# Three halves of an adaLN conditioning, from TensorE's products to GpSimd's multiplies and adds

## The chip, the cores and the metric

The kernel is one program on one NeuronCore of a Trainium2 chip. The metric is the time of one execution on the device in microseconds (us), the median of several runs. Besides, one execution was recorded by the hardware profiler, which gives each engine's instructions with their start and duration. The engines are TensorE (PE), VectorE (DVE), ScalarE (ACT), GpSimd (POOL) and SyncE (SP), which only starts DMA transfers here. Each has a queue of its own that it works off in order; an instruction that has to wait for another engine or a transfer holds up all that stands behind it in its queue.

## The reference

A decoder trunk with two layers, 256 tokens, 1024 features, one sequence, float32. Each layer has a mixer (layer 0: two kinds of softmax attention, groups A and B, of eight heads each) and a gated FFN, both between norms. What the layers add is set by a conditioning vector c: for each layer one product of 1024 x 6144 gives six vectors of 1024.

```python
cond = jax.nn.silu(c)                                     # 1 x 1024
for layer in range(DEPTH):
    mod = cond @ ada_w[layer] + ada_b[layer]              # 1 x 6144
    shift_m, scale_m, gate_m, shift_f, scale_f, gate_f = [m[:, None, :] for m in jnp.split(mod, 6, axis=-1)]
    h = rmsnorm(x, mix_pre_g[layer]) * (1.0 + scale_m) + shift_m
    y = even_mixer(h, ...) if layer % 2 == 0 else odd_mixer(h, ...)
    x = x + gate_m * rmsnorm(y, mix_post_g[layer])
    h = rmsnorm(x, ffn_pre_g[layer]) * (1.0 + scale_f) + shift_f
    y = conv_ffn(h, ffn_w_up[layer], ffn_conv_w[layer], ffn_conv_b[layer], ffn_w_down[layer])
    x = x + gate_f * rmsnorm(y, ffn_post_g[layer])
```

The 24 MB of `ada_w` of a layer are read once, for a product with a single row.

## The kernel before

The weights of the conditioning are worked off in halves of 512 columns. A half is named by its first column: 2048 and 2560 are gate_m, 3072 and 3584 shift_f, 4096 and 4608 scale_f, 5120 and 5632 gate_f. One half is four transfers of 128x2x512 (512 KB each, `ada_load`, L143, tiles aw_2048_0 to aw_2048_3), so eight row tiles of 128x512. The tiles go through a pool `aw` of four buffers: a load waits until the reader of the tile four before has finished. Only 5632 has buffers elsewhere (tag `qkv`).

There are two ways to work off a half. By products (p, `ada_main`, L151): eight matmuls, each with a padded conditioning column cpad (128x32) as weights, four row groups of TensorE side by side; each takes two passes, so that the profile counts 16; ScalarE then copies the rows out (L158, or L270 for a gate). On VectorE (v, `ada_sum`, L195 and L197): the first row tile times its 128 values of the conditioning, then seven times multiply and add in one operation, into acc, which keeps a sum for each partition. Either way, a shift or scale is turned by four transposes on TensorE (L167) so that a feature has a partition of its own, reduced over the rest by VectorE (L168) and gets its bias (L171) and gain (L174): `ada_keep`, which writes mod. A gate is needed on all partitions: one matmul with a matrix of ones (L272) sums it and spreads it, and VectorE multiplies the gain on (L274).

Which half is worked off how and behind which point of the program stands in the table ADA_AT; `more_ada(point)` is called behind each pair of heads and each projection. Halves of kind v are put on a list, and `step_aside` issues a few of their steps at a time between VectorE's other work. The gate of the FFN, 5120 and 5632, is not in the table: its products fill TensorE's waits at the boundary between mixer and FFN (`gate_halves`, L276).

The boundary (`boundary`, L375 to L464) takes the mixer's result y0m, two tiles of 128 tokens by two halves of features. For the first token tile: squares on ScalarE (L331), root on GpSimd (L335, L336: rpm); VectorE multiplies with the gate (ygm, L388), adds it to the trunk (xr, L392); squares and root again (rnm); xnm (L406); TensorE turns it (xTm, L414); ScalarE and VectorE apply scale and shift (hsm, L422 and L424), and the result is split into two parts hh (L427) and hl (L431). The same for the second token tile, interleaved. The first product of the FFN is u (L473), with weights rawu that are split by ScalarE and VectorE (L311, L312) into wu.

The order of the instructions on each engine is set when the program is built, by a scheduler that plays the program through with estimated times and takes what is ready first. Inside the boundary the order of VectorE, ScalarE, GpSimd and TensorE is as the lines are written, yet steps of the conditioning may be scheduled between them. SP's order is as written for the first part of the program, and set by the scheduler from the attention on.

## Time and profile before

| | |
|---|---|
| median of 3 runs | 692.56 us |
| fastest, slowest run | 691.07, 694.53 us |
| span of the profiled execution | 690.2 us |
| busy, TensorE / VectorE | 672.1 us / 525.3 us |
| busy, ScalarE / GpSimd | 369.8 us / 32.7 us |

The span runs from the first to the last instruction of the profiled execution. The profile gives no other time of that execution than its span. Layer 0's attention lies between about 60 and 161 us, the boundary in front of the FFN between 161 and 176 us, and the FFN of layer 0 from there on. The granted clock of TensorE is 1.00 in all the stretches shown below, the higher of its two levels.

### The profile page before, as it was taken

Reading aid. Unit: us, or ns where it says so; the run is one execution under the profiler, and the core shown is the slowest. Engines: PE = TensorE matmul, PEld = TensorE weight load, DVE = VectorE, ACT = ScalarE, POOL = GpSimd, SP = SyncE. Lnnn points to the kernel's source line nnn. Section 1 sums busy time; section 2 is a strip of 40 time slices with the busy share of each in tenths; the row PEclk is TensorE's granted clock in tenths of the full one; section 3 lists DMA queues with packets and bytes.
Section 4 is the critical chain, followed back from the end, with each engine's and each line's share of the span. In section 5 each row is a group of like instructions: output and inputs, shape, how many; then the busy total and the mean of one; then the engine's idle time right before and its main releaser. Section 6 shows DMA issues by size and latency. Waiting matters only on the chain.

```text
span 690.2 us, 11782 instructions
## 1 busy us (share of the span) xinstructions
PE 672.1 (97%) x4547; PEld 573.6 (83%) x4547; DVE 525.3 (76%) x1008; ACT 369.8 (54%) x645; POOL 32.7 (5%) x95
## 2 busy tenths in 40 slices
PE   8899999999999999999999999999999999999996
PEld 6667986476899999999986998767599999999994
DVE  1553577688899999999978787774788777777775
ACT  3433464835565555555655645864565555555552
POOL 2000000001000000000001002410200000000000
PEclk9999999999999999999999999999999999999998
DMA  7999986996858878888875867622266555555511
GB/s 256 352 368 360 221 307 240 326 348 223 294 194 290 277 257 297 264 258 277 285 270 184 290 225 266 210 82 88 75 190 237 185 183 183 183 184 188 191 49 62
DMA packets 100819, 159.12 MB, mean 231 GB/s; under 512 B 4087, under 2 KB 62611, under 8 KB 100763
## 3 DMA queue, kind: packets, MB, share of 16 engines
q1 hardware_dynamic: 100739, 158.35, 69.2%
q8 instruction: 36, 0.59, 0.3%
q14 instruction: 20, 0.16, 0.1%
q10 hardware_dynamic: 24, 0.02, 0.0%
HBM read 156.52 MB, written 1.84 MB: 229 GB/s over the span
## 4 chain that ended last, share of the span: by engine, by line
PE 88%; DVE 5%; ACT 2%; DMA 1%; issue 1%; POOL 1%; SPq 1%; DVEq 0%; POOLq 0%; ACTq 0%
PE u L473 36%; PE y1f L688 9%; PE y0f L688 9%; PE psb L473 3%; PE psd L473 3%; PE y1m L688 2%; PE y0m L688 2%; PE psa_q L809 2%; PE psa_k L809 2%; PE ada_first L151 2%; PE ada L151 1%; DMA aw_first<-in_ada_w 1%; PE sab L600 1%; PE sab L592 1%; PE sab L572 1%
## 5 line engine op out<-in xcount | busy, mean ns | idle before, releaser
L737 ACT ACTIVATE cv<-u,cvT 128x256 f32<-128x256 f32 x88 | 49.1, 560 | 65.3 <-PE u L473 61.4
L473 PE MATMUL u<-hh,wu_0h 128*128 128x256 f32 x352 | 69.8, 280 | 1.2 <-DVE hh L427 1.2
L473 PE MATMUL u<-hh,wu_1h 128*128 128x256 f32 x352 | 70.0, 280 | 0.0
L473 PE MATMUL u<-hh,wu_1l 128*128 128x256 f32 x352 | 69.9, 279 | 0.0
L473 PE MATMUL u<-hh,wu_0l 128*128 128x256 f32 x352 | 69.5, 279 | 0.0
L311 ACT CAST wu_1h<-rawu 128x1024 fp32r<-128x1024 f32 x44 | 46.2, 1051 | 31.1 <-PE y1f L688 17.6
L738 DVE SCALAR_TENSOR_TENSOR cv<-u,cvT,cv 128x255 f32<-128x255 f32 x88 | 42.0, 478 | 27.1 <-ACT cv L737 27.0
L473 PEld LDWEIGHTS u<-hh,wu_0h 128*128 128x128 f32 x352 | 54.8, 188 | 4.2 <-PE ada L272 1.4
L195 DVE SCALAR_TENSOR_TENSOR acc<-aw,cpad,acc 128x512 f32<-128x512 f32 x77 | 57.6, 749 | 0.4
L312 DVE TENSOR_TENSOR wu_0l<-rawu,wu_0h 128x1024 fp32r<-128x1024 f32 x44 | 53.5, 1221 | 5.3 <-ACT wu_0h L311 5.3
L311 ACT CAST wu_0h<-rawu 128x1024 fp32r<-128x1024 f32 x44 | 46.0, 1046 | 19.0 <-PE u L473 18.9
L312 DVE TENSOR_TENSOR wu_1l<-rawu,wu_1h 128x1024 fp32r<-128x1024 f32 x44 | 53.6, 1217 | 3.0 <-ACT wu_1h L311 2.9
L473 PEld LDWEIGHTS u<-hh,wu_1h 128*128 128x128 f32 x352 | 53.7, 188 | 0.0
L473 PEld LDWEIGHTS u<-hh,wu_1l 128*128 128x128 f32 x352 | 53.7, 188 | 0.0
L473 PEld LDWEIGHTS u<-hh,wu_0l 128*128 128x128 f32 x352 | 53.5, 188 | 0.0
L473 PE MATMUL u<-hl,wu_1h 128*128 128x256 f32 x352 | 48.2, 279 | 0.0
L473 PE MATMUL u<-hl,wu_0h 128*128 128x256 f32 x352 | 48.2, 279 | 0.0
L311 ACT CAST wd_0h<-rawd 128x1024 fp32r<-128x1024 f32 x26 | 27.3, 1049 | 35.2 <-PE u L473 31.7
L473 PEld LDWEIGHTS u<-hl,wu_1h 128*128 128x128 f32 x352 | 44.2, 188 | 0.0
L473 PEld LDWEIGHTS u<-hl,wu_0h 128*128 128x128 f32 x352 | 44.2, 188 | 0.0
L740 DVE SCALAR_TENSOR_TENSOR cv<-u,cvT,cv 128x254 f32<-128x254 f32 x88 | 41.7, 477 | 1.4
L312 DVE TENSOR_TENSOR wd_0l<-rawd,wd_0h 128x1024 fp32r<-128x1024 f32 x26 | 31.7, 1221 | 13.4 <-ACT wd_0h L311 13.2
(556 smaller groups left out, 1566.0 us busy)
## 6 DMA issues: line engine op xcount, KB each, us to landing
rawu<-in_ffn_w_up SPq DMA_DIRECT2D x44, 1024.0 KB, 5.2
aw<-in_ada_w SPq DMA_DIRECT2D x80, 512.0 KB, 6.7
rawd<-in_ffn_w_down SPq DMA_DIRECT2D x22, 1024.0 KB, 5.1
aw_first<-in_ada_w SPq DMA_DIRECT2D x32, 256.0 KB, 5.1
rawaqk<-in_ab_w_in SPq DMA_DIRECT2D x8, 512.0 KB, 6.7
rawb<-in_ab_w_in SPq DMA_DIRECT2D x4, 1024.0 KB, 8.7
rawd<-in_cd_w_in SPq DMA_DIRECT2D x4, 1024.0 KB, 5.8
rawc<-in_cd_w_in SPq DMA_DIRECT2D x4, 544.0 KB
```

The source lines that it names most:

```text
L151: last_main[:] = [nc.tensor.matmul(ps[32 * j:32 * j + 32, 0:cols], cpad[:, k, :], ws[k // 2][:, k % 2, 0:cols], start=(k < 4), stop=(k >= ...
L195: nc.vector.scalar_tensor_tensor(acc, w, c_k, acc, op0=ALU.mult, op1=ALU.add)
L311: nc.scalar.copy(hi, src)
L312: low = nc.vector.tensor_tensor(lo, src, hi.bitcast(F32), op=ALU.subtract)
L473: nc.tensor.matmul(dst(f), w[:, k, f * P:(f + 1) * P], h[:, 4 * u + k, :], start=(u == 0 and first(f) and f not in seen), stop=(u == 1 and ...
L572: nc.tensor.matmul(ps[:, P:3 * P], q[:, P:S], k, start=True, stop=True)
L592: nc.tensor.transpose(self.ps[j][:, b * P:(b + 1) * P], lt[:, b * P:(b + 1) * P], ident)
L688: last_down[:] = [nc.tensor.matmul(ys[t][:, h, :], g[p // 2][:, t * P:(t + 1) * P], wu[p % 2][:, h * 512:(h + 1) * 512], start=start and p ...
L737: nc.scalar.activation(tt[:, s, :], u_ps, AF.Identity, bias=cvT[:, bcol:bcol + 1], scale=col(2))
L738: nc.vector.scalar_tensor_tensor(tt[:, s, 1:S], u_ps[:, 0:S - 1], col(1), tt[:, s, 1:S], op0=ALU.mult, op1=ALU.add)
L740: nc.vector.scalar_tensor_tensor(tt[:, s, 2:S], u_ps[:, 0:S - 2], col(0), tt[:, s, 2:S], op0=ALU.mult, op1=ALU.add)
L809: nc.tensor.matmul((pq, pk)[f // 4][:, f % 4 // 2, f % 2 * S:(f % 2 + 1) * S], w[:, f * P:(f + 1) * P], h[:, kk, :], start=(kk == 0 and f ...
```

## The change

The kind p of the table is replaced by a kind g: the eight row tiles are summed on GpSimd. GpSimd multiplies the first row tile by its conditioning column into acc; each further row tile is multiplied in place, in its aw buffer, and then added to acc: eight multiplies and seven adds of 128x512 for each half. The halves are 2048, 2560 (gate) and 3072 (shift) of layer 0. What follows is what kind v had already: the transposes and the reduction over 128 partitions, or the product with ones. The steps are issued at once, not between VectorE's work. `ada_part` and `ada_cols` go; comments go too, and with them line numbers move by up to 14.

```diff
 ADA_AT = {
-    "a0": [("p", 0, 2, 0)],
+    "a0": [("g", 0, 2, 0)],
     "a1": [("v", 0, 4, 0)],
-    "a3": [("p", 0, 2, 1), ("p", 0, 3, 0)],
+    "a3": [("g", 0, 2, 1), ("g", 0, 3, 0)],
     "bv": [("v", 0, 4, 1)],
     "b3": [("v", 0, 3, 1)],
...
-    def ada_part(layer, c0, ws):
-        ps = bank(f"ada_{layer}_{c0}", "a")
-        ada_main(ps, ws)
-        part = small(f"part_{layer}_{c0}", tag="part")
-        nc.scalar.copy(part, ps)
-        return ps, part
...
-    def ada_sum(acc, ws):
+    def ada_sum(acc, ws, engine):
         for k in range(KT):
             yield
             w, c_k = ws[k // 2][:, k % 2, :], cpad[:, k, 0:1]
-            if k:
-                nc.vector.scalar_tensor_tensor(acc, w, c_k, acc, op0=ALU.mult, op1=ALU.add)
+            if not k:
+                engine.tensor_scalar_mul(acc, w, c_k)
+            elif engine is nc.vector:
+                engine.scalar_tensor_tensor(acc, w, c_k, acc, op0=ALU.mult, op1=ALU.add)
             else:
-                nc.vector.tensor_scalar_mul(acc, w, c_k)
+                engine.tensor_scalar_mul(w, w, c_k)
+                engine.tensor_tensor(acc, acc, w, op=ALU.add)
...
-        yield from ada_sum(acc, ws)
+        yield from ada_sum(acc, ws, engine)
...
-    def ada_cols(layer, which, h, gain=None):
-        columns_for(layer, which)
-        c0 = which * D + h * 512
-        ps, part = ada_part(layer, c0, ada_load(layer, c0))
-        ada_keep(layer, which, 4 * h, ps, part, range(4), gain)
...
-        if on_vector:
+        if engine:
             brow = small(f"brow_{layer}_{c0}", (1, 512), tag="t")
             nc.scalar.dma_start(brow, ada_b[layer:layer + 1, c0:c0 + 512])
-            yield from ada_sum(part, ws)
+            yield from ada_sum(part, ws, engine)
...
         for kind, layer, which, h in ADA_AT.get(point, ()):
+            engine = nc.vector if kind == "v" else nc.gpsimd
             if which == 2:
-                gate = ada_gate(layer, which, h, mix_post_g, on_vector=kind == "v")
-                if kind == "v":
-                    aside.append(gate)
-                else:
-                    list(gate)
-                continue
-            args = (layer, which, h, {1: MIX_G, 4: FFN_G}.get(which))
+                steps = ada_gate(layer, which, h, mix_post_g, engine=engine)
+            else:
+                steps = ada_vector(layer, which, h, {1: MIX_G, 4: FFN_G}.get(which), engine)
             if kind == "v":
-                aside.append(ada_vector(*args))
+                aside.append(steps)
             else:
-                ada_cols(*args)
+                list(steps)
```

The scheduler then orders the engines anew. On SP, the loads of the conditioning in front of the boundary stood like this before (each row is a line, the tile written, its source and, in brackets, the queues and engines whose signals it waits for; DMAHW is an earlier transfer):

```order
L304 DMA rawu_0_1_1797<-in_ffn_w_up 128x8x256 [waits DMAHW1_49,DVE_49]
L143 DMA aw_4608_0_1284<-in_ada_w 128x2x512 [waits DMAHW3_49,DMAHW2_49,PE_49]
L143 DMA aw_4608_1_1286<-in_ada_w 128x2x512 [waits DMAHW4_49,PE_49]
L143 DMA aw_4608_2_1288<-in_ada_w 128x2x512 [waits DMAHW5_49,PE_49]
L143 DMA aw_4608_3_1290<-in_ada_w 128x2x512 [waits DMAHW6_49,PE_49]
L304 DMA rawu_1_0_1937<-in_ffn_w_up 128x8x256 [waits DMAHW7_49,DVE_49]
L143 DMA aw_3584_0_1616<-in_ada_w 128x2x512 [waits DMAHW3_49,DMAHW0_49,DVE_49]
L143 DMA aw_3584_1_1618<-in_ada_w 128x2x512 [waits DMAHW4_49,DMAHW1_49,DVE_49]
L143 DMA aw_3584_2_1620<-in_ada_w 128x2x512 [waits DMAHW5_49,DMAHW2_49,DVE_49]
```

and stand like this in the changed program:

```order
L290 DMA rawu_1_0_1959<-in_ffn_w_up 128x8x256 [waits DMAHW7_49,DVE_49]
L143 DMA aw_3072_1_952<-in_ada_w 128x2x512 [waits DMAHW0_49,Pool_49]
L143 DMA aw_3072_2_954<-in_ada_w 128x2x512 [waits DMAHW1_49,Pool_49]
L143 DMA aw_3072_3_956<-in_ada_w 128x2x512 [waits DMAHW2_49,Pool_49]
L143 DMA aw_5632_0_1675<-in_ada_w 128x2x512 [waits DMAHW3_49,PE_49]
L143 DMA aw_5632_1_1677<-in_ada_w 128x2x512 [waits DMAHW4_49]
L143 DMA aw_5632_2_1679<-in_ada_w 128x2x512 [waits DMAHW5_49,DVE_49]
L143 DMA aw_4608_0_1306<-in_ada_w 128x2x512 [waits DMAHW6_49,Pool_49]
L143 DMA aw_4608_1_1308<-in_ada_w 128x2x512 [waits DMAHW6_49,DMAHW0_49,DVE_49]
L143 DMA aw_5632_3_1681<-in_ada_w 128x2x512 [waits DMAHW1_49,PE_49]
L290 DMA rawu_1_1_1961<-in_ffn_w_up 128x8x256 [waits DMAHW2_49,DVE_49]
L143 DMA aw_4608_2_1310<-in_ada_w 128x2x512 [waits DMAHW3_49,Pool_49]
```

All of 4608 stood in front of 3584, waiting for TensorE; now the tiles of 3072 stand in front, waiting for GpSimd (Pool), 4608_0 waits for GpSimd and 4608_1 for VectorE. Further behind, the loads of 3584 and 5120 now wait for VectorE's sums, and the last of these is the last tile of 5120:

```order
L143 DMA aw_3584_0_1638<-in_ada_w 128x2x512 [waits DMAHW5_49,DMAHW0_49,DVE_49]
L143 DMA aw_3584_1_1640<-in_ada_w 128x2x512 [waits Pool_49]
L143 DMA aw_3584_2_1642<-in_ada_w 128x2x512 [waits DMAHW7_49,DMAHW3_49,DVE_49]
L143 DMA aw_3584_3_1644<-in_ada_w 128x2x512 [waits DMAHW4_49,DVE_49]
L143 DMA aw_5120_0_1662<-in_ada_w 128x2x512 [waits DMAHW5_49,DMAHW1_49,DVE_49]
L143 DMA aw_5120_1_1664<-in_ada_w 128x2x512 [waits DMAHW6_49,DMAHW2_49,DVE_49]
L143 DMA aw_5120_2_1666<-in_ada_w 128x2x512 [waits DMAHW7_49,DVE_49]
L143 DMA aw_5120_3_1668<-in_ada_w 128x2x512 [waits DMAHW0_49,DVE_49]
```

In before these too waited for VectorE (the first piece shows it for 3584), yet for sums that it made ahead of the boundary, and 5632 stood among them.

On VectorE, the beginning of the boundary before, from the last two sums of 3584 to the second pair of xr:

```order
L195 SCALAR_TENSOR_TENSOR acc_3584_1624<-aw_3584_3_1622,cpad,acc_3584_1624 128x512
L388 TENSOR_TENSOR ygm_0_0_1668<-y0m_0_1473,gate_2_764 128x512
L388 TENSOR_TENSOR ygm_0_1_1669<-y0m_1_1474,gate_2_764 128x512
L392 SCALAR_TENSOR_TENSOR xr<-ygm_0_0_1668,rpm_0_1678,xr 128x512
L392 SCALAR_TENSOR_TENSOR xr<-ygm_0_1_1669,rpm_0_1678,xr 128x512
L406 TENSOR_SCALAR xnm_0_0_1692<-xr,rnm_0_1689 128x512
L406 TENSOR_SCALAR xnm_0_1_1694<-xr,rnm_0_1689 128x512
L388 TENSOR_TENSOR ygm_1_0_1670<-y0m_0_1475,gate_2_764 128x512
L168 TENSOR_REDUCE mod_3_933<-ada_3584_1633 128x4
L388 TENSOR_TENSOR ygm_1_1_1671<-y0m_1_1476,gate_2_764 128x512
L171 TENSOR_TENSOR mod_3_933<-mod_3_933,vT 128x4
L392 SCALAR_TENSOR_TENSOR xr<-ygm_1_0_1670,rpm_1_1700,xr 128x512
```

and in the changed program, from ygm on, and then, eight rows further, up to the norm of the second token tile:

```order
L374 TENSOR_TENSOR ygm_0_0_1690<-y0m_0_1495,gate_2_764 128x512
L374 TENSOR_TENSOR ygm_0_1_1691<-y0m_1_1496,gate_2_764 128x512
L190 SCALAR_TENSOR_TENSOR acc_4608_1314<-aw_4608_2_1310,cpad,acc_4608_1314 128x512
L378 SCALAR_TENSOR_TENSOR xr<-ygm_0_0_1690,rpm_0_1700,xr 128x512
L378 SCALAR_TENSOR_TENSOR xr<-ygm_0_1_1691,rpm_0_1700,xr 128x512
L190 SCALAR_TENSOR_TENSOR acc_4608_1314<-aw_4608_2_1310,cpad,acc_4608_1314 128x512
L190 SCALAR_TENSOR_TENSOR acc_4608_1314<-aw_4608_3_1312,cpad,acc_4608_1314 128x512 x2
L392 TENSOR_SCALAR xnm_0_0_1714<-xr,rnm_0_1711 128x512
L392 TENSOR_SCALAR xnm_0_1_1716<-xr,rnm_0_1711 128x512
L161 TENSOR_REDUCE mod_3_949<-ada_3072_974 128x4
L188 TENSOR_SCALAR acc_3584_1646<-aw_3584_0_1638,cpad 128x512
```

```order
L190 SCALAR_TENSOR_TENSOR acc_3584_1646<-aw_3584_1_1640,cpad,acc_3584_1646 128x512
L164 TENSOR_TENSOR mod_4_829<-mod_4_829,vT 128x4
L190 SCALAR_TENSOR_TENSOR acc_3584_1646<-aw_3584_1_1640,cpad,acc_3584_1646 128x512
L167 SCALAR_TENSOR_TENSOR mod_4_829<-mod_4_829,vT 128x4
L190 SCALAR_TENSOR_TENSOR acc_3584_1646<-aw_3584_2_1642,cpad,acc_3584_1646 128x512 x2
L190 SCALAR_TENSOR_TENSOR acc_3584_1646<-aw_3584_3_1644,cpad,acc_3584_1646 128x512 x2
L161 TENSOR_REDUCE mod_3_949<-ada_3584_1655 128x4
L164 TENSOR_TENSOR mod_3_949<-mod_3_949,vT 128x4
L410 TENSOR_SCALAR hsm_0_1_1760<-xTm_0_1_1730,mod_4_829,mod_3_949 128x128 x2
L413 CAST hh<-hsm_0_0_1757 128x4x128
L392 TENSOR_SCALAR xnm_1_0_1777<-xr,rnm_1_1767 128x512
L392 TENSOR_SCALAR xnm_1_1_1779<-xr,rnm_1_1767 128x512
```

Behind ygm_0 now stand the last four sums of 4608 and all of 3584, and with them the reductions and adds that make mod_3 and mod_4; xnm_1_0, which stood behind hsm_0 and the first cast before, stands behind all of these.

On TensorE, the transposes of xnm_1_0 (xTm_1) stand behind the products of 5120 and 5632 in both programs. Before:

```order
L414 MATMUL xTm_0_0_1707<-ident,xnm_0_1_1694 128x128 x2
L414 MATMUL xTm_0_1_1708<-ident,xnm_0_1_1694 128x128 x2
L151 MATMUL ada_5120_1652<-aw_5120_0_1640,cpad 32x512 x2
L151 MATMUL ada_5120_1652<-aw_5120_1_1642,cpad 32x512 x2
L151 MATMUL ada_5120_1652<-aw_5120_2_1644,cpad 32x512 x2
L151 MATMUL ada_5120_1652<-aw_5120_3_1646,cpad 32x512 x2
L151 MATMUL ada_5632_1663<-aw_5632_0_1653,cpad 32x512 x2
L151 MATMUL ada_5632_1663<-aw_5632_1_1655,cpad 32x512 x2
L151 MATMUL ada_5632_1663<-aw_5632_2_1657,cpad 32x512 x2
L151 MATMUL ada_5632_1663<-aw_5632_3_1659,cpad 32x512 x2
L272 MATMUL ada_5120_1652<-part_5120_1650,ones 128x512
L414 MATMUL xTm_1_0_1709<-ident,xnm_1_0_1755 128x128 x2
```

and in the changed program:

```order
L160 MATMUL ada_4608_1341<-ident,acc_4608_1314 128x128 x4
L160 MATMUL ada_3584_1655<-ident,acc_3584_1646 128x128 x4
L151 MATMUL ada_5120_1674<-aw_5120_0_1662,cpad 32x512 x2
L151 MATMUL ada_5120_1674<-aw_5120_1_1664,cpad 32x512 x2
L151 MATMUL ada_5120_1674<-aw_5120_2_1666,cpad 32x512 x2
L151 MATMUL ada_5120_1674<-aw_5120_3_1668,cpad 32x512 x2
L151 MATMUL ada_5632_1685<-aw_5632_0_1675,cpad 32x512 x2
L151 MATMUL ada_5632_1685<-aw_5632_1_1677,cpad 32x512 x2
L151 MATMUL ada_5632_1685<-aw_5632_2_1679,cpad 32x512 x2
L151 MATMUL ada_5632_1685<-aw_5632_3_1681,cpad 32x512 x2
L261 MATMUL ada_5120_1674<-part_5120_1672,ones 128x512
L400 MATMUL xTm_1_0_1731<-ident,xnm_1_0_1777 128x128 x2
```

The transposes of 4608 and 3584 have come in between those of xnm_0 and the products of 5120.

## Rows read from the trace of the kernel before

**Rows 1.** The page: engine, busy us, share of the span, instructions.
```profile
PE 672.1 (97%) x4547; PEld 573.6 (83%) x4547; DVE 525.3 (76%) x1008; ACT 369.8 (54%) x645; POOL 32.7 (5%) x95
```

**Rows 2.** The page: busy tenths of GpSimd in 40 slices of 17.3 us.
```profile
POOL 2000000001000000000001002410200000000000
```

**Rows 3.** Chain of waits, 60 to 182 us: start, us, what.
```profile
92.84 1.85 PE ada L151 x16
...
120.53 1.85 PE ada L151 x16
...
130.40 1.84 PE ada L151 x12
...
132.72 0.98 PE ada L151 x4
...
172.59 0.75 POOL rnm L336
```

**Rows 4.** TensorE's timeline at the boundary: start, busy us, what, idle before.
```profile
169.36 3.64 PE L151 MATMUL ada<-aw,cpad 128*32 128x512 f32 x32 [0.43 <-DVE mod L168]
172.93 1.12 PE L272 MATMUL ada<-part,ones 128*128 128x512 f32 x2
173.90 1.09 PE L414 MATMUL xTm<-ident,xnm 128*128 128x128 f32 x8
...
176.40 0.50 PE L473 MATMUL u<-hh,wu_0h 128*128 128x256 f32 x2 [0.55 <-DVE hh L427]
```

**Rows 5.** Stretches: span; busy us (count) of PE, PEld, DVE, ACT, POOL; clock; DMA share; GB/s.
```profile
200.00:365.00 165.00, 163.27 (x1150) 151.94 (x1148) 152.96 (x264) 89.15 (x128) 1.72 (x4) 1.00 0.82 269
```

**Rows 6.** GpSimd's groups: count, busy us, mean ns, idle before.
```profile
L961 POOL TENSOR_TENSOR qt<-rpq 128x64 f32<-128x64 f32 x4 | 1.3, 320 | 1.8 <-DVE rpq L958 1.8
...
L962 POOL TENSOR_TENSOR kr<-rpk 128x16 f32<-128x16 f32 x2 | 0.4, 218 | 0.0
L883 POOL TENSOR_SCALAR_AFFINE_SELECT causal<-causal 128x256 f32<-128x256 f32 x1 | 0.4, 399 | 0.0
...
masks.py:199 POOL TENSOR_SCALAR_AFFINE_SELECT ident<-ident 128x128 f32<-128x128 f32 x1 | 0.3, 293 | 0.0
```

**Rows 7.** Line 195: count, ns min/median/max, first and last start.
```profile
L195 DVE SCALAR_TENSOR_TENSOR acc<-aw,cpad,acc x77: 727/744/889, 98.7 to 432.7; 128x512 f32<-128x512 f32 x77
```

**Rows 8.** Line 335, the same columns.
```profile
L335 POOL TENSOR_SCALAR rpf<-sspf x4: 299/300/752, 360.6 to 684.8; 128x1 f32<-128x1 f32 x4
```

**Rows 9.** SP's timeline, 125 to 165 us.
```profile
131.42 2.69 SPq L143 DMA_DIRECT2D aw<-in_ada_w  x4
...
158.07 3.92 SPq L143 DMA_DIRECT2D aw<-in_ada_w  x2
```

**Rows 10.** Tile aw, 45 to 182 us: ns min/median/max; transfers.
```profile
L195 DVE SCALAR_TENSOR_TENSOR acc<-aw,cpad,acc x21: 727/743/752, 98.7 to 160.9; 128x512 f32<-128x512 f32 x21
L197 DVE TENSOR_SCALAR acc<-aw,cpad x3: 481/482/486, 97.8 to 149.1; 128x512 f32<-128x512 f32 x3
...
DMA to landing us min/median/max: 4.1/7.0/8.6
```

**Rows 11.** VectorE's timeline at the boundary.
```profile
162.24 1.38 DVE L388 TENSOR_TENSOR ygm<-y0m,gate 128x512 f32<-128x512 f32 x2 [0.65 <-ACT junkpm L331]
163.97 1.41 DVE L392 SCALAR_TENSOR_TENSOR xr<-ygm,rpm,xr 128x512 f32<-128x512 f32 x2 [0.35 <-POOL rpm L336]
167.22 0.89 DVE L406 TENSOR_SCALAR xnm<-xr,rnm 128x512 f32<-128x512 f32 x2 [1.83 <-POOL rnm L336]
...
168.62 0.68 DVE L168 TENSOR_REDUCE mod<-ada 128x4 f32<-128x512 f32 x1
...
169.82 0.15 DVE L171 TENSOR_TENSOR mod<-mod,vT 128x4 f32<-128x4 f32 x1
...
173.36 0.88 DVE L406 TENSOR_SCALAR xnm<-xr,rnm 128x512 f32<-128x512 f32 x2 [0.45 <-POOL rnm L336]
```

More of the change, by code (lines that the diff above doesn't have):

```diff
@@ L152, in ada_main, with ada_keep @@
                                              start=(k < 4), stop=(k >= 4), tile_position=(0, 32 * j))]
-    def ada_part(layer, c0, ws):
-        ps = bank(f"ada_{layer}_{c0}", "a")
-        ada_main(ps, ws)
-        part = small(f"part_{layer}_{c0}", tag="part")
-        nc.scalar.copy(part, ps)
-        return ps, part
-    def ada_keep(layer, which, k0, ps, part, blocks, gain, per=4):
+    def ada_keep(layer, which, k0, ps, part, blocks, gain, per):
         n = len(blocks)
@@ L193, in ada_sum, with ada_vector @@
             w, c_k = ws[k // 2][:, k % 2, :], cpad[:, k, 0:1]
-            if k:
-                nc.vector.scalar_tensor_tensor(acc, w, c_k, acc, op0=ALU.mult, op1=ALU.add)
-            else:
-                nc.vector.tensor_scalar_mul(acc, w, c_k)
-    def ada_vector(layer, which, h, gain):
+            if not k:
+                engine.tensor_scalar_mul(acc, w, c_k)
+            elif engine is nc.vector:
+                engine.scalar_tensor_tensor(acc, w, c_k, acc, op0=ALU.mult, op1=ALU.add)
+            else:
+                engine.tensor_scalar_mul(w, w, c_k)
+                engine.tensor_tensor(acc, acc, w, op=ALU.add)
+    def ada_vector(layer, which, h, gain, engine):
         columns_for(layer, which)
@@ L243, in ada_first_load, with ada_gate @@
         return w
-    def ada_gate(layer, which, h, post_g, tag="aw", on="a", on_vector=False):
+    def ada_gate(layer, which, h, post_g, tag="aw", on="a", engine=None):
         c0 = which * D + h * 512
```

## The prediction

> **What bounds the kernel now.** I read the busy shares first. TensorE is busy 672.1 of 690.2 us, VectorE 525.3, GpSimd 32.7 [rows 1], and GpSimd's slices are empty from the second to the ninth, 17 to 155 us [rows 2]. Then the chain of waits, from 60 to 182 us, where the change lies. It runs on TensorE almost without a break up to 161.5 us, and the four pieces of it that carry the products of the three halves are to be seen there by their line: 1.85, 1.85, 1.84 and 0.98 us [rows 3]. So they are on the path, and a product taken away lets everything behind it move up. From 162 to 176 us the chain changes hands: ScalarE's squares, VectorE's norm and modulation, GpSimd's root [rows 3], until u, the FFN's first product, starts at 176.40 [rows 4]. That start is the figure to follow: from 200 to 365 us TensorE is busy 163.27 of 165.00 us [rows 5], and the order of the instructions there is the same in both kernels, so that a start that comes late by some microseconds has at most 1.7 us in which to be made good. The change is decided by when u starts.
>
> **What is removed.** 48 products of 128x512, 1.85 + 1.85 + 1.84 + 0.98 = 6.52 us, all on the chain [rows 3], and three copies on ScalarE, which is no part of the chain there. The product with ones of each gate, and the four transposes of the shift, stay. If nothing else moved, the time would be 692.6 - 6.5 = 686.0.
>
> **What is added on GpSimd.** 24 multiplies and 21 adds of 128x512. No row of before has either at that size. Nearest rows [rows 6]: an add-like operation of two inputs takes 0.320 us at 64 columns and 0.218 at 16, an operation of one input 0.293 at 128 and 0.399 at 256. From below: each no dearer than the largest seen, 24 x 0.40 + 21 x 0.32 = 16 us. From above: in proportion to the columns, 24 x 1.17 + 21 x 2.56 = 82 us. I take the slopes between the rows, 2.1 and 0.83 ns a column, as both rows of a pair are of one kind: an add 1.27, a multiply 0.61, 14.6 + 26.7 = 41 us in all, nearly 14 us for a half. GpSimd has from about 58 to 150 us for it and nothing else to do [rows 2], so 41 us hide beside TensorE and 82 would not.
>
> A rule speaks against this cover. In the rows, a GpSimd operation of 0.300 us takes 0.752 in the longest of its four executions, and the longest of VectorE's 77 sums 0.889 against 0.744 [rows 7, 8]: something is shared. The Trainium skill, SBUF — State Buffer, section "Who interferes with whom", says that VectorE and GpSimd share one pair of ports, held by one of them for the whole instruction. By it the 45 operations would wait behind VectorE's two-input ones, up to 0.74 us each, 33 us more; that is the case of the late GpSimd below.
>
> **What moves: the loads.** All weights of the conditioning go through four buffers (aw). TensorE empties a buffer at once; GpSimd holds each for three or four operations. The scheduler has answered this by its order. On SP, the loads of 4608 stood ahead of everything of 3584; now three tiles of 3072 wait for GpSimd in front, and 4608_0 behind the last add of 2560; the loads of 3584 and 5120 now wait for VectorE's sums of 4608 and of 3584, tile by tile. In before 4608 was issued from 131.42 on, and the last tile of 5120 in the pair that ends at 161.99 [rows 9]. By my prices GpSimd is through with 2560 at about 139 (its last multiplies wait for a tile) and with 3072 at about 149, so 4608_0 lands about 144, 4608_2 about 154.
>
> **What moves: VectorE.** In before all sums stand ahead of ygm, the first step of the boundary. Now four of 4608 and all eight of 3584 stand behind it. Sums last 0.743, the first of a half 0.482 [rows 10]: 11 x 0.743 + 0.482 = 8.66 us. In before ygm starts at 162.24 and the shift (mod) is done at 169.97, 7.73 later [rows 11]. In the new order there come into that stretch: 8.66 of sums; two more reductions, 2 x 0.68 = 1.36; their adds, 2 x 0.15 = 0.3; the second pair of xr, 1.41, and two of hsm, about 0.7, which stood behind it; and the way over TensorE's transposes, 0.6. Out of it goes the wait for rnm, 1.83, as there is work in it now; 0.35 stays [rows 11]. So the shift is done at 7.73 + 8.66 + 1.36 + 0.3 + 1.41 + 0.7 + 0.6 - 1.83 = 18.9 us after ygm, and the last sum at 17.5. xnm of the second token tile, which started 173.36 - 162.24 = 11.1 after ygm, starts at 18.9 + 0.7 + 0.4 = 20.0: 9 us more.
>
> **What moves: TensorE's wait.** In front of the transposes of that tile (xTm at 173.90, 11.66 after ygm) stand the products of the gates 5120 and 5632, 3.64 us for both, and one with ones, 0.56 [rows 4]. In before they hide under VectorE's work. Now the last tile of 5120 is issued only when the last sum of 3584 has freed its buffer, 17.5 after ygm; a tile lands 4.1 us after its issue at the least, 7.0 in the median [rows 10]; then a quarter of 5120's products, all of 5632's and the ones: 0.46 + 1.82 + 0.56 = 2.8. Transposes at 17.5 + 4.1 + 2.8 = 24.4, or 27.3 by the median: 12.7 to 15.6 us later against ygm than before. I take 13, near the lower, as SP has nothing else to send by then. Queued behind these products on TensorE are the transposes and all of the FFN, so the whole wait counts.
>
> **The sum.** ygm comes earlier by the removed 6.5 less what TensorE loses in waits for GpSimd's sums and late loads; I give that 1 us, so -5.5 (the ends are -6.5, nothing lost, and -3). The boundary grows by 13 (9 if 5120 is not late, 15.6 by the median). -5.5 + 13 = +7.5. The profiled execution has a span of 690.2 us, 2.4 under the median of the runs; no other time of it is given. 690.2 + 7.5 = 697.7 span, so 700.1 as a median: I say 700. Its own range, from -6.5 + 12 to -4.5 + 15.6, is 698 to 704.
>
> **Rivals.**
> GpSimd is late (chance 0.14). If its operations wait for VectorE as in the rows of 0.752 and 0.889, the half 3072 ends at about 160 instead of 149, as 15 operations after the last load of it cost 0.7 more each. The load of 4608_2 waits for it; VectorE needs it 1.4 us after ygm, at about 158, and would stand there until 166. Some 6 us of this is not covered: 692.6 + 7.5 + 6 = 706. For it: the two outliers [rows 7, 8]. Against it: they are the longest of 81, and GpSimd hardly ran beside VectorE in before, so the rows say little either way.
> A wash (chance 0.19). The tiles of 5120 land in time, so VectorE's 9 us alone lengthen the boundary, against -6: +3, 695.5. For it: nothing but these tiles is then on SP, and three of four are asked for earlier. Against it: even the shortest landing is 4.1 us.
> Faster (chance 0.12). VectorE absorbs its sums at the boundary. The point is between ygm and xnm: if the sums run at the start-to-start pace of a pair, 1.41 - 0.74 = 0.67, and fill the waits of 1.83, 0.35 and 0.45 [rows 10, 11], they add 11 x 0.67 + 0.4 - 2.6 = 5.2, and the reductions fall into waits for TensorE. The products give 6.5, the FFN's 1.7 us of waits come back [rows 5], and so do TensorE's 0.43 and 0.55 in front of it [rows 4]: 692.6 + 5.2 - 6.5 - 1.7 - 1.0 = 688.6. It decides for this when the boundary grows by less than 3 us, which needs the last tile of 5120 on its way within 8 us of ygm. Against it: the tile's buffer is freed by the last sum.
> That the change does nothing, because the products were hidden: against it stands that all four pieces are on the chain; its time would lie in the wash.
>
> **How the numbers follow.** Forecast 0.55, late GpSimd 0.14, wash 0.19, faster 0.12. The time is the forecast's, 700. What can be told from no change is 0.5%, 3.5 us: under 689.1 is faster, over 696.0 slower. Slower: forecast and late GpSimd, 0.69. The same: the wash, and some of the faster case that ends above 689.1, 0.21. Faster: 0.10. A range of 8 in 10 takes the wash and the forecast whole, the faster case in part and the late GpSimd up to 707: 690.5 to 707.
>
> **What would show it.** In the profile of the changed kernel: GpSimd busy about 41 us more, in two stretches before 150; no product of 2048, 2560 and 3072 on the chain; y0m and ygm 5 to 6 us earlier; between ygm and xnm on VectorE twelve sums, and the shift about 19 us after ygm; TensorE waiting first for VectorE's last sum and then some 4 us for aw before the last products of 5120; u at 183 to 184 and the FFN behind it as long as before. I am wrong if u starts before 180, if the sums of GpSimd take more than 60 us, or if the stretch from u to the end changes by more than 2 us.

## The result, and the profile after

The changed kernel takes 709.63 us (708.03 to 710.51, four runs) beside 691.82 us of the kernel before (four runs too) on the same chip: ratio 1.0242, interval 1.0211 to 1.0272. That is 17.8 us slower. I had forecast 700, in 690.5 to 707: a loss of 7.5 us.

The page of the changed kernel, with the rows that answer to [rows 1, 2], and TensorE's granted clock in the same 40 slices:

```profile
PE 672.9 (95%) x4499; PEld 575.4 (81%) x4499; DVE 538.6 (76%) x1010; ACT 368.3 (52%) x642; POOL 109.9 (16%) x140
...
POOL 2007729782000000000002000530100000000000
PEclk9999999798699999999999999999999999999999
```

GpSimd has 77.2 us more, in slices 4 to 10, and TensorE 0.8 us more [rows 1] in spite of the missing products: its granted clock falls in slices 8, 10 and 11, and a piece of a product that took 0.592 us in before takes 1.06 at the lower level (the median of the 32 pieces of 5120 and 5632). The chain of waits from the end of the attention to u (start, us, what):

```profile
143.72 1.01 DVE ltab L575
...
145.10 5.72 DMA aw<-in_ada_w
...
150.85 0.48 DVE acc L188
...
157.85 0.05 SPq L290
...
157.99 9.10 DMA aw<-in_ada_w
...
167.85 0.76 DVE xr L378
...
183.05 1.10 PE ada L160 x4
...
195.31 4.70 PE u L459 x38
```

In before the attention's end was TensorE's work, up to the last products of y0m:

```profile
158.04 3.46 PE y0m L688 x14
```

Now two transfers of aw stand in the chain, of 5.72 and 9.10 us, and TensorE comes into it again only at 183. u starts at 195.31 instead of 176.40 [rows 4], 18.9 us later, and the span is 18.6 us longer (708.8 instead of 690.2): what is lost is lost before u, and behind it only 0.3 us is given back. VectorE at the boundary, the columns as in [rows 11]:

```profile
155.19 2.31 DVE L298 TENSOR_TENSOR wo0c_1l<-rawo0c,wo0c_1h 128x1024 fp32r<-128x1024 f32 x1
...
161.78 1.37 DVE L374 TENSOR_TENSOR ygm<-y0m,gate 128x512 f32<-128x512 f32 x2
167.18 0.75 DVE L190 SCALAR_TENSOR_TENSOR acc<-aw,cpad,acc 128x512 f32<-128x512 f32 x1 [4.02 <-DMA aw<-in_ada_w]
167.85 1.41 DVE L378 SCALAR_TENSOR_TENSOR xr<-ygm,rpm,xr 128x512 f32<-128x512 f32 x2
169.17 2.32 DVE L190 SCALAR_TENSOR_TENSOR acc<-aw,cpad,acc 128x512 f32<-128x512 f32 x3
...
179.79 3.12 DVE L190 SCALAR_TENSOR_TENSOR acc<-aw,cpad,acc 128x512 f32<-128x512 f32 x4
```

ygm starts at 161.78, 0.46 us earlier than before. Right behind it the fifth sum of 4608 stands still for 4.02 us until its tile, 4608_2, has landed, and xr, whose operands were ready (GpSimd had written rpm by 163.49), waits behind it. The last sum ends at 179.79 + 3.12 = 182.91. TensorE behind it, answering to [rows 4]:

```profile
183.05 1.09 PE L160 MATMUL ada<-ident,acc 128*128 128x128 f32 x4 [7.75 <-DVE acc L190]
184.92 7.10 PE L151 MATMUL ada<-aw,cpad 128*32 128x512 f32 x32 [0.78 <-DVE mod L161]
...
192.92 1.04 PE L400 MATMUL xTm<-ident,xnm 128*128 128x128 f32 x8
...
195.31 0.50 PE L459 MATMUL u<-hh,wu_0h 128*128 128x256 f32 x2 [0.49 <-DVE hh L413]
```

The 32 pieces of the products of 5120 and 5632 take 7.10 us instead of 3.64; their weight loads (PEld) show that the last tile of 5120 came at 187.79, 4.9 us after the last sum:

```profile
186.48 0.34 PEld L151 LDWEIGHTS ada<-aw,cpad 128*32 128x32 f32 x4 [1.36 <-DMA aw<-in_ada_w]
187.79 0.19 PEld L151 LDWEIGHTS ada<-aw,cpad 128*32 128x32 f32 x6 [0.97 <-DMA aw<-in_ada_w]
```

By stretches (columns as in [rows 5]):

```profile
120.00:140.00 20.00, 15.48 (x60) 8.54 (x58) 16.02 (x57) 11.93 (x41) 15.70 (x11) 0.74 0.63 203
176.00:183.00 7.00, 0.00 (x0) 0.00 (x0) 6.80 (x13) 0.01 (x1) 0.00 (x0) 0.50 0.50 149
186.00:190.00 4.00, 4.00 (x19) 1.24 (x18) 1.92 (x5) 1.43 (x5) 0.84 (x2) 0.50 0.85 274
200.00:365.00 165.00, 165.00 (x1212) 156.25 (x1211) 155.43 (x262) 90.84 (x123) 0.00 (x0) 1.00 0.81 271
```

From 120 to 140 us, in the attention, TensorE is busy 15.48 of 20 us at a granted clock of 0.74; from 176 to 183 it does nothing, and the products from 186 to 190 run at 0.50, the lower of its two levels (1.2 GHz). The FFN is as forecast, without gaps. GpSimd's new work, shortest, median and longest in ns:

```profile
L192 POOL TENSOR_SCALAR aw<-aw,cpad x21: 1557/1577/2690, 59.1 to 146.7; 128x512 f32<-128x512 f32 x21
```
```profile
L193 POOL TENSOR_TENSOR part<-part,aw x14: 1260/1303/2327, 68.0 to 139.0; 128x512 f32<-128x512 f32 x14
L193 POOL TENSOR_TENSOR acc<-acc,aw x7: 1262/1292/2152, 125.3 to 154.3; 128x512 f32<-128x512 f32 x7
```

An add takes 1.26 to 1.30 us, as I had it (1.27); a multiply takes 1.56 at its shortest, where I had 0.61.

### The profile page after: what moved, and what is told of

The parts are those of the page before. It is cut to its first block, busy times and chain, and to the rows that moved or that the text cites. A ratio compares the mean times of both kernels' runs of the same rounds, so it can differ in the third digit from the quotient of the medians.

```text
span 708.8 us, 11745 instructions
## 1 busy us (share of the span) xinstructions
PE 672.9 (95%) x4499; PEld 575.4 (81%) x4499; DVE 538.6 (76%) x1010; ACT 368.3 (52%) x642; POOL 109.9 (16%) x140
## 4 chain that ended last, share of the span: by engine, by line
PE 82%; DVE 7%; DMA 5%; ACT 3%; issue 2%; SPq 1%; POOL 1%; DVEq 0%; POOLq 0%; ACTq 0%
PE u L459 35%; PE y1f L674 8%; PE y0f L674 8%; PE psb L459 3%; PE psd L459 3%; PE y1m L674 2%; DMA aw<-in_ada_w 2%; PE psa_q L795 2%; PE psa_k L795 2%; PE ada L151 2%; PE ada_first L151 1%; DVE acc L190 1%; DMA rawav<-in_ab_w_in 1%; PE sab L586 1%; DMA aw_first<-in_ada_w 1%
## 5 line engine op out<-in xcount | busy, mean ns | idle before, releaser
L297 ACT CAST wu_1h<-rawu 128x1024 fp32r<-128x1024 f32 x44 | 46.3, 1052 | 31.1 <-PE y1f L674 17.6
L321 POOL TENSOR_SCALAR rpf<-sspf 128x1 f32<-128x1 f32 x4 | 1.6, 404 | 378.1 <-ACT junkpf L317 378.1
L298 DVE TENSOR_TENSOR wu_0l<-rawu,wu_0h 128x1024 fp32r<-128x1024 f32 x44 | 53.6, 1221 | 5.2 <-ACT wu_0h L297 5.2
L298 DVE TENSOR_TENSOR wu_1l<-rawu,wu_1h 128x1024 fp32r<-128x1024 f32 x44 | 53.6, 1218 | 3.0 <-ACT wu_1h L297 3.0
L297 ACT CAST wu_0h<-rawu 128x1024 fp32r<-128x1024 f32 x44 | 46.1, 1047 | 18.9 <-PE u L459 18.9
```

The costliest lines, as they stand in the source:

```text
L297: nc.scalar.copy(hi, src)
L298: low = nc.vector.tensor_tensor(lo, src, hi.bitcast(F32), op=ALU.subtract)
L321: nc.gpsimd.tensor_scalar(r, ss[:, 0:1], ss[:, 1:2], EPS, op0=ALU.add, op1=ALU.add)
```

## The experiments

The ratio is always to the kernel before, run on the same chip, with its 95% interval.

**The products alone.** Does TensorE's saving in the attention count?

Four of the eight products of each of the three halves are left out (n is 4 there), and nothing stands in their place; the loads stay.

```diff
-        for k in range(KT):
+        for k in range(n):
...
-                                             start=(k < 4), stop=(k >= 4), tile_position=(0, 32 * j))]
+                                             start=(k < 4), stop=(k >= n - 4), tile_position=(0, 32 * j))]
```

> The kernel before with four of the eight products of each of the three halves 2048, 2560 and 3072 left out (half of the contraction is missing); nothing runs on GpSimd in their place. My theory of the path (what TensorE no longer does there makes all behind it earlier): half of 6.52 us, so -3.3: 689 us, ratio 0.995. Rival (the attention is as much bound by VectorE's and ScalarE's chain of softmax steps, and time taken from TensorE there comes back as its waits): ratio 0.998 to 1.002, and TensorE's busy time between 100 and 160 us falls short of the stretch by some 3 us.

693.47 us, ratio 1.0019 (0.9995 to 1.0042): nothing is won. Its u starts at 176.41, before's at 176.40. TensorE from 120 to 140 us, and its waits from 100 to 162 us (who waits for whom: us, times, longest):

```profile
120.00:140.00 20.00, 17.49 (x95) 10.11 (x95) 14.99 (x57) 13.77 (x41) 0.00 (x0) 0.91 1.08 301
```
```profile
PE sab L600 <- ACT ptsab L595: 1.3, 2, 0.7
PE sab L570 <- DVE oTab L679: 1.2, 1, 1.2
```

In before TensorE had 20.00 busy in that stretch, at a clock of 1.00, and no wait. The products filled places in which the softmax on ScalarE and VectorE was not ready; without them, of the 3.3 us that they took, 2.5 come back as waits, and the clock falls to 0.91. The rival holds.

**GpSimd's work beside the old kernel.** The same 45 operations, on a tile that nobody reads, at the loads of 2048, 2560 and 3072:

```diff
+    def pool_work(w):
+        nc.gpsimd.tensor_copy(dum[:, 0:1], w[:, 0, 0:1])
+        for k in range(KT):
+            nc.gpsimd.tensor_scalar_mul(dum, dum, cpad[:, k, 0:1])
+            if k:
+                nc.gpsimd.tensor_tensor(dum, dum, dum, op=ALU.add)
```

> The kernel before with its products on TensorE, and beside them the work of the change on GpSimd as idle work: at the load of 2048, 2560 and 3072 eight multiplies and seven adds of 128x512 on a tile of their own, that nobody reads. The order of the other engines is as before but for a handful of rows, and no load waits for this work. Ports theory (GpSimd and VectorE hold each other up: in the changed kernel the normalisation of the attention's weights, 128x256, takes 0.73 us in the mean instead of 0.35): the attention's end moves from 161.5 to 166 or more, the whole to 697 to 700 us, and the same rows of VectorE grow as in the changed kernel. Buffers theory (all of the loss comes from aw tiles that GpSimd holds too long): 691 to 693 us, as before.

698.0 us, ratio 1.0056 (1.0025 to 1.0087): some 4 us, of the 17.8, and within the range of the ports theory. In its trace ygm starts at 163.76, 1.5 us later than in before, and u at 181.18, 17.4 us behind ygm instead of 14.2. A rest of the idle work stands between GpSimd's two steps of the root there, and xr waits 1.92 us for rpm, where it waited 0.35 [rows 11]:

```profile
167.05 2.18 DVE L404 SCALAR_TENSOR_TENSOR xr<-ygm,rpm,xr 128x512 f32<-128x512 f32 x2 [1.92 <-POOL rpm L348]
```

So in this trace 1.5 of the 4.8 us by which u is late come from the attention, and the rest from the boundary. A second kernel puts 45 fills (`memset`) of that tile in the place of the 15 operations of a half:

> The kernel before with GpSimd only writing: at the load of each of the three halves 45 fills of a 128x512 tile that nobody reads, of 0.52 us, some 71 us in all, none reads an operand. If GpSimd and VectorE collide over reading: VectorE's normalisation of 128x256 stays at 0.35 us (0.51 beside the multiplies and adds), 692 us. If any work on GpSimd holds VectorE up: 0.45 us and more, 695 to 698 us.

694.09 us, ratio 1.0015 (0.9993 to 1.0037): not to be told from no change. Yet VectorE's normalisation, which has one input, is held up by either, 0.346 us in before; its subtraction for the split, which has two, only by the work that reads. Before, then beside the multiplies and adds, then beside the fills (count, busy us, mean ns):

```profile
L590 DVE TENSOR_SCALAR ltab<-ltab,stab 128x256 f32<-128x256 f32 x8 | 2.8, 346 | 0.0
...
L312 DVE TENSOR_TENSOR wo0c_0l<-rawo0c,wo0c_0h 128x1024 fp32r<-128x1024 f32 x2 | 2.4, 1220 | 0.5 <-ACT wo0c_0h L311 0.5
```
```profile
L602 DVE TENSOR_SCALAR ltab<-ltab,stab 128x256 f32<-128x256 f32 x8 | 4.1, 508 | 0.0
...
L324 DVE TENSOR_TENSOR wo0c_0l<-rawo0c,wo0c_0h 128x1024 fp32r<-128x1024 f32 x2 | 3.0, 1516 | 0.3 <-ACT wo0c_0h L323 0.3
```
```profile
L600 DVE TENSOR_SCALAR ltab<-ltab,stab 128x256 f32<-128x256 f32 x8 | 4.0, 495 | 0.0
...
L322 DVE TENSOR_TENSOR wo0c_0l<-rawo0c,wo0c_0h 128x1024 fp32r<-128x1024 f32 x2 | 2.4, 1224 | 0.0
```

The lines are taken from one execution each, that of the fills from one of its slowest (697.99 us). So the engines do hold each other up, and it is the smaller part of the loss.

**How many halves.** Only 2048 on GpSimd, then 2048 and 2560 (`"a3": [("g", 0, 2, 1), ("p", 0, 3, 0)]`):

> Only 2048 on GpSimd, which runs beside the projections of group B; 2560 and 3072 by products on TensorE as before. Buffers theory: the loads of 4608 wait for TensorE again and nearly all sums stand ahead of the boundary, so the 1.85 us of its products are won: 690 to 691 us. Ports theory: most of VectorE's work there is splitting weights with two inputs, which GpSimd holds up as well; 692 to 694 us.

> 2048 and 2560 on GpSimd, 3072 by products on TensorE. The order has six of the sums of 3584 in the boundary. Order theory: the boundary is 5 to 8 us longer, the attention not shorter, since 2560's share of GpSimd stands beside it: 696 to 702 us. Buffers theory: the loads of 4608 and 3584 no longer wait for GpSimd's 3072, so the wait for 4608_2 at xr (4.0 us) and most of the rest goes: 691 to 695 us.

692.45 us, ratio 0.9964 (0.9936 to 0.9993), and 701.48 us, ratio 1.0114 (1.0088 to 1.0140). The first half is a small gain; the second takes 1.5% and the third, by the changed kernel's ratio, another 1.3%. 701.48 is at the end of what the order theory gave and out of what the buffers theory gave: u starts 186.17 - 165.58 = 20.6 us after ygm although no load waits for GpSimd's 3072.

**A cheap multiply, and a fifth buffer.** First seven of the eight multiplies of each half over 16 of the 512 columns, the rest of their work left out:

```diff
-                engine.tensor_scalar_mul(w, w, c_k)
+                engine.tensor_scalar_mul(w[:, 0:16], w[:, 0:16], c_k)
```

> The changed kernel with GpSimd's in-place multiplies over 16 of the 512 columns: seven eighths of the multiplies' work is left out, the adds stay. GpSimd's work falls from 77 to about 45 us, near the price that I had forecast. The order then has all sums of 4608 and 3584 ahead of the boundary. Price theory (the dear multiply, 1.58 us, holds the tiles too long): u starts as in the kernel before less what the products give, 687 to 692 us. Ports theory: the adds still stand beside the attention, some half of the loss in it stays: 690 to 695 us. If it stays over 700, it is neither.

694.79 us, ratio 1.0009 (0.9985 to 1.0033); u at 176.33. With the buffers free sooner all sums stand ahead of ygm and the boundary's loss is gone, as the price theory had it. The 6.5 us are not won either: the time lies above its range, whose lower end, 687, was that gain, and within that of the ports theory (690 to 695), so the time alone does not decide between the two. TensorE's waits do say where the gain went: 5.3 us of them from 60 to 163 us, against 0.3 in before.

```diff
-BUFS = {"raw": 4, "whi": 4, "wlo": 4, "aw": 4, "gate": 2, "qkv": 8, "t": 13, "o": 8, "part": 2, "brow": 2,
+BUFS = {"raw": 4, "whi": 4, "wlo": 4, "aw": 5, "gate": 2, "qkv": 8, "t": 12, "o": 8, "part": 2, "brow": 2,
```

> The changed kernel with five aw buffers instead of four, and twelve instead of thirteen of the small work tiles. The loads run one tile further ahead of GpSimd; the order has all sums of 4608 and three of 3584 ahead of ygm. Buffers theory: the wait for 4608_2 is gone and the boundary is 5 to 8 us shorter, the whole 698 to 703 us; the loss in the attention (GpSimd beside VectorE) stays. If the boundary's length comes from the clock and from GpSimd's roots alone: 707 to 710 us.

697.89 us, ratio 1.0067 (1.0042 to 1.0093), with GpSimd's dear work unchanged: nearly three quarters of the loss go with one buffer more, a little more than I had expected. The control:

> The kernel before with five aw buffers and twelve small work tiles, the control for the changed kernel with five. If the buffers held before back too, under 690 us; else 691 to 694 us, and the 697.9 us of the changed kernel with five are then 5 us of loss that the buffers do not mend (GpSimd beside VectorE, and three sums at the boundary).

693.12 us, ratio 1.0003 (0.9983 to 1.0023): the buffer is worth nothing where TensorE empties it.

**Position or lateness.** What my sum rested on, without GpSimd: the sums of 3584 put into the boundary of the kernel before.

```diff
+            in_m0 = name == "m0"
+            late_sums(2 * in_m0)
+            steps((mul_y, 1, 0), (mul_y, 1, 1))
+            late_sums(in_m0)
+            steps((add_y, 1, 0), (add_y, 1, 1))
             xT = y_tiles(f"xT{name}")
             turn_x(0)
+            late_sums(99 * in_m0)
+            if in_m0:
+                next(fill[0])
...
```

`late_sums` issues steps of the sum of 3584, the last call all that are left; next(fill[0]) then starts the loads of 5120.

> The kernel before, all products on TensorE, GpSimd without the new work; only the eight sums of 3584 are put into the boundary on VectorE, about where the changed kernel has them, and the loads of 5120 behind them. Order theory (what my sum rests on: the sums and the loads behind them lengthen the boundary even if GpSimd costs nothing): last sum 13.4 us after ygm, last tile of 5120 landed 4.1 to 7 us later, the second tile's transposes 8 to 11 us later against ygm than before, u at 184 to 187, the whole 699 to 703 us. Rival (the sums fill waits of VectorE, and the boundary of the changed kernel is long because GpSimd makes loads late): under 695 us.

717.0 us, ratio 1.0345 (1.0306 to 1.0383), beyond both ranges. ygm came late, at 173.33, since this edit also draws 4608 together in front of the boundary and TensorE waits 10.0 us for its sum; that part says nothing on the question, and so the whole time says nothing. From ygm to u, however, it is 199.81 - 173.33 = 26.5 us, against 14.2 in before: 12.3 more, with the second tile's transposes 24.0 after ygm, against 11.66. So the position alone, of the sums and of the loads behind them, makes the boundary that much longer (the granted clock is 0.50 from 185 to 195 us there, as in the changed kernel from 183 to 190). The reverse, in the changed kernel: only the order of VectorE put back.

```diff
-            nc.vector.tensor_mul(yg[t, half], ys[t][:, half, :], g[:, cols(half)])
+            with tc.issue_after(last_sum[0].ins) if name == "m0" and (t, half) == (0, 0) else nullcontext():
+                nc.vector.tensor_mul(yg[t, half], ys[t][:, half, :], g[:, cols(half)])
```

> The changed kernel with one thing fixed in the order: ygm of the first token tile stands behind VectorE's last sum of 3584, so that all sums stand ahead of the boundary as in before; the loads and GpSimd's work keep the changed kernel's order. Position theory (the boundary is long because sums stand inside it): the boundary is back at 14 to 17 us and the whole at 696 to 702 us. Lateness theory (the sums can't run earlier, since their tiles, which wait behind GpSimd's buffers, land from 150 to 180 us): ygm waits until about 178 us, u starts at 193 to 197 as in the changed kernel or later, 708 to 714 us.

707.71 us, ratio 1.0206 (1.0177 to 1.0235): at the lower end of the lateness theory (708 to 714) and far from the position theory (696 to 702). VectorE ahead of ygm, and u:

```profile
166.24 3.11 DVE L190 SCALAR_TENSOR_TENSOR acc<-aw,cpad,acc 128x512 f32<-128x512 f32 x4 [5.02 <-DMA aw<-in_ada_w]
...
173.22 3.12 DVE L190 SCALAR_TENSOR_TENSOR acc<-aw,cpad,acc 128x512 f32<-128x512 f32 x4
176.25 1.28 DVE L375 TENSOR_TENSOR ygm<-y0m,gate 128x512 f32<-128x512 f32 x2
```
```profile
192.60 0.50 PE L460 MATMUL u<-hh,wu_0h 128*128 128x256 f32 x2 [0.49 <-DVE hh L414]
```

The boundary is short again, 192.60 - 176.25 = 16.4 us, but the last sum ends at 173.22 + 3.12 = 176.34 though nothing of the boundary stands in front of it. In before the last one had ended at 160.85 + 0.74 = 161.59, ahead of ygm at 162.24 [rows 11]:

```profile
160.85 0.74 DVE L195 SCALAR_TENSOR_TENSOR acc<-aw,cpad,acc 128x512 f32<-128x512 f32 x1
```

So the sums end 14.8 us late: VectorE waits 5.02 us for the tile of the fifth sum of 4608, and from 166.24 on it works without a gap.

**The clock.** 30 products that nobody reads, in TensorE's wait at the boundary:

```diff
             turn_x(0)
+            for _ in range(30 if name == "m0" else 0):
+                nc.tensor.matmul(gate_ps[1][:, 0:P], ones, ones, start=True, stop=True)
```

> The changed kernel with 30 products of 128x128 that nobody reads on TensorE, behind the transposes of the first token tile at the boundary in front of the first FFN, where it waits some 8 us for VectorE's last sum. Clock theory: the products of 5120 and 5632 and the one with ones behind them ran at the lower clock (granted 0.50 from 172 to 190 us, a product 1.06 us instead of 0.59); with the clock up, u starts 2 to 3 us earlier and the whole takes 706 to 708 us. If only the last tile's landing sets that end: 709 to 710 us, as the changed kernel.

710.08 us, ratio 1.0227 (1.0179 to 1.0275), too wide to tell. So again, with the changed kernel itself beside it:

> The changed kernel with TensorE kept busy at the boundary, timed in more rounds beside the changed kernel itself. Clock theory: the products behind the wait took 2.3 us more at the lower clock, so 0.3% faster than the changed kernel of the same rounds, ratio to before 1.020 to 1.022. If the last tile's landing covers it: no difference, 1.024.

> The changed kernel once more, as the measure for the one with TensorE kept busy: 1.024 of before, as measured (1.021 to 1.027).

Ratios 1.0257 (1.0232 to 1.0282) and 1.0242 (1.0213 to 1.0270): no gain. The granted clock is 1.00 from 183 to 190 us now, and the products wait for their tiles instead:

```profile
186.59 1.05 PE L151 MATMUL ada<-aw,cpad 128*32 128x512 f32 x4 [1.19 <-DMA aw<-in_ada_w]
188.82 2.77 PE L151 MATMUL ada<-aw,cpad 128*32 128x512 f32 x20 [1.18 <-DMA aw<-in_ada_w]
```

At the boundary the low clock is a mark of the wait, not a cause of the loss. What the 0.74 from 120 to 140 us costs was not tried.

**The same halves on VectorE, and a version that is faster.** All three halves as kind v:

> The three halves summed on VectorE, one operation of 0.74 us a row tile, instead of on GpSimd: 24 operations, 17.6 us more on VectorE, no GpSimd, all sums of 4608 and 3584 ahead of ygm in the order. Price theory (a buffer is held 1.5 us instead of 5 to 6, so the loads stay early): the boundary stays at 14 us; the attention is 0 to 8 us longer since VectorE has 67 us of work in 100 to 180 us already; 692 to 700 us. If the sums are the burden whoever makes them: 703 us and more.

693.15 us, ratio 1.0011 (0.9983 to 1.0039): 24 operations that hold a buffer shortly cost nothing, and win nothing. Without any new work on GpSimd TensorE waits 5.3 us from 60 to 166 us. And 2048 alone on GpSimd, with five buffers:

> Only 2048 on GpSimd, and five aw buffers: all sums stand ahead of ygm. The one half alone measured 0.996 of before. Buffers theory: the sum that stood behind ygm and the wait for loads go, 688 to 690 us. If the attention is filled by TensorE's products anyway, nothing is to be had: 691 to 693 us.

688.7 us, ratio 0.9934 (0.9908 to 0.9960): faster than both kernels, with ygm at 161.41 and u at 175.16. It is 0.7% (4.4 us) below before with five buffers; in the two traces u is 1.3 us earlier (176.48 there), of the 1.85 that the products of 2048 took, and the rest is not explained. VectorE's normalisation is not held up in it:

```profile
L592 DVE TENSOR_SCALAR ltab<-ltab,stab 128x256 f32<-128x256 f32 x8 | 2.8, 348 | 0.0
```

The share of 2048 is done before most of the softmax begins. That this is why it wins was not tried apart.

## Why the prediction was wrong

Point by point, with u's delay against before as the measure (forecast 7.5, measured 18.9 us):

| step | forecast | measured |
|---|---|---|
| ygm against before | -5.5 | -0.5 |
| last sum after ygm | 17.5 | 182.91 - 161.78 = 21.1 |
| from it to the second tile's transposes | 4.1 + 2.8 = 6.9 | 192.92 - 182.91 = 10.0 |
| transposes against before (11.66) | +13 | 31.1 - 11.66 = +19.5 |

Of the 11.4 us by which u came later than forecast, 5.0 arose in front of ygm, 3.6 from ygm to the last sum and 3.1 behind it (my sum had rounded 12.7 up to 13, which takes off the other 0.3). The upper end of the sum's own range, 704, counts 4.5 us gained in front of ygm, where my worst case was 3; with 3 it is 705, still under the measured time.

The step that failed is the first: "they are on the path, and a product taken away lets everything behind it move up". The four pieces stood on the chain because TensorE never waited there, and it never waited because they filled it. With half of the products left out and nothing else changed, u starts at the same time. I allowed 1 us of loss on 6.5; it was 6. TensorE's waits show it: they come to 5.8 us from 60 to 162 us, against 0.3 in before. The three longest (us, times, longest):

```profile
PE sab L578 <- DVE ltab L575: 1.9, 2, 1.7
PE sab L556 <- DVE oTab L665: 1.2, 1, 1.2
PE sab L578 <- DVE ltab L576: 0.8, 1, 0.8
```

VectorE's normalisation (ltab), for which TensorE waits here, is itself held up beside GpSimd (0.726 us in the mean instead of 0.346). The kernel that has these collisions alone lost 1.5 us in front of ygm, some 4 in all, and it had the products; with the halves on VectorE and no such collisions the waits were 5.3 us. How the two add up in the changed kernel was not taken apart.

The second is a price: the multiply, 0.61 by the slope of two rows, measured 1.56 at its shortest. GpSimd took 77 us more instead of 41, near my upper bound of 82, and over the 60 that I had named as a sign of being wrong. I took the slope of an operation with a pattern instead of a multiply by a column for the same kind.

By my timetable GpSimd was through with 2560 at 139 and with 3072 at 149, 4608_0 landed at 144 and 4608_2 at 154. GpSimd was through at 138.99 + 1.30 = 140.29 and 148.20 + 8.22 = 156.42, and the tiles landed at 150.82 and 167.1:

```profile
138.99 1.30 POOL L193 TENSOR_TENSOR part<-part,aw 128x512 f32<-128x512 f32 x1
...
148.20 8.22 POOL L193 TENSOR_TENSOR acc<-acc,aw 128x512 f32<-128x512 f32 x5
```

So the price is not all of it. By GpSimd 4608_0 was free to go at 140.29, and it went at 145.10: loads of 5632 stand in front of it on SP, and the waits of that queue from 131 to 147 us are theirs:

```profile
SPq L143 <- PE sab L578: 10.8, 1, 10.8
SPq L143 <- DVE ltab L575: 2.0, 1, 2.0
```

4608_1 went at 153.06, when the second sum of 4608_0 had ended (151.85 + 1.19 = 153.04): the other three buffers were held for 3072. 4608_2, the 4.02 us in front of xr, went at 157.99, when GpSimd had been through with all of 3072 for 1.6 us. It stood right behind a load of the FFN's weights (SP's L290 in the chain), which was sent when VectorE's split L298 had ended at 155.19 + 2.31 = 157.50. That split took 2.31 us instead of 1.22, yet in before it ended hardly earlier, at 156.12 + 1.22 = 157.34, and the load behind it went at 157.36:

```profile
157.36 0.37 SPq L304 DMA_DIRECT2D rawu<-in_ffn_w_up  x1
```

What is new is that 4608, which had gone from 131.42 on [rows 9], stands behind these waits. A queue in which a load stands behind another's wait was in my order rows, and I priced no wait there.

The moved sums and the load of 5120 behind them were right as a mechanism and in order (12.3 us for 3584's alone, without GpSimd, against 8 to 11 expected). But the loss does not rest on them alone: put ahead again, with the loads as they were, they gain back some 0.4 of 2.4%, within the two intervals' overlap. Lateness of the tiles is enough by itself for most of it, and position lengthens the boundary by itself; what frees the buffers sooner removes both (a cheap multiply, VectorE's single operation) or nearly three quarters of the loss (a fifth buffer). These three kernels also have another order of loads and sums, as the scheduler makes it anew. So the runs show that the slow reader of the buffers is at the root. They do not show how much of the loss comes from the time a buffer is held and how much from the order that was set for it; GpSimd's work with the loads in their old order was not tried.

The rival of the late GpSimd (706, chance 0.14) is the nearest to the time, and its place, a sum of 4608 waiting behind ygm for its tile, is where 4.02 us were lost. Its cause, GpSimd held up by VectorE, is the smaller part. At the shortest times of its operations GpSimd's work is 24 x 1.557 + 21 x 1.260 = 63.8 us, against the 41 forecast; of the 77 measured some 13 are left for being held up (an estimate from these rows), where the rival had 33. Operations held up on both engines are in the traces of the changed kernel and of the one with idle work. The Trainium skill, SBUF — State Buffer, section "Who interferes with whom", says in finer words than I used that a one-input operation of VectorE in its fast form collides with any work of GpSimd, and one with two inputs only with its reads; this agrees with 0.495 us beside fills for the former, and 1.22 beside fills and 1.52 beside reads for the latter. That the normalisation runs in that form no run here shows.

The landing of the last tile of 5120, forecast at 4.1 us, took 4.9. The rest of the 10.0 holds TensorE at its lower clock, which, as the runs with it kept up show, was not there to be won.

## What to carry to other kernels

An engine that is busy without a gap can be busy with filler: before a cut of its work is counted, leave the work out and see whether the end moves. When a reader of a buffer gets slower, follow the buffer, not the reader: count how long each tile is held, which load takes it next, and what stands behind that load in its queue. Engines with spare time are worth using where nothing near them is late; here that held for the first half, and not for the two behind it.

## What the runs showed of the hardware

On GpSimd a multiply of 128x512 by a column (1.56 us at its shortest) costs more than an add of two such tiles (1.26), and VectorE does both in one operation of 0.74. A fill of that size takes 0.53 in the mean of 135:

```profile
L145 POOL MEMSET dum<- 128x512 f32 x135 | 71.9, 533 | 7.7
```

VectorE's one-input operation between tiles of SBUF (the normalisation, 0.346 us) is slowed by any of GpSimd's work, 0.495 us in the mean beside fills and 0.508 beside multiplies and adds; its two-input subtraction of 1.22 us is not slowed beside fills, and takes 1.52 beside multiplies and adds.
